# A decoder block on one Trainium2 core: weaving column chunks at stage seams, sums moved from GpSimd to VectorE, and a new order of the sine tables

## The chip, the cores and the metric

The kernel runs on one core of a Trainium2 chip. The core has a matmul engine (TensorE, PE in the profile, with its weight loads PEld), VectorE (DVE), ScalarE (ACT), GpSimd (POOL) and a queue engine for transfers (SP). Each engine works through its own instructions in order and waits on semaphores for the others. The metric is device time in microseconds, the median of several runs; lower is better.

## The reference

One layer of a hybrid decoder block, with batch 1, 256 tokens, width 2048, all in float32:

```
xn   = rms_norm(x)
proj = xn @ w_in                      # 2048 x 11264: u_s5, u_lru, q, k, v, gate logits
g_s5, g_lru, g_attn = split(sigmoid(gate_logits + b_gate))
y_s5   = s5_branch(u_s5, ...)         # complex diagonal scan, gelu, y * sigmoid(y @ w_glu + b)
y_lru  = rglru_branch(u_lru, ...)     # causal conv, two gates, h = a*h + sqrt(1-a^2)*(i*x)
y_attn = stick_breaking_attention(q, k, v)
merged = g_s5*(y_s5 @ w_br_s5) + g_lru*(y_lru @ w_br_lru) + g_attn*(y_attn @ w_br_attn)
h   = x + merged @ w_out
hn  = rms_norm(h)
h   = h + relu(hn @ w_up)**2 @ w_down # width 8192 between
out = rms_norm(h)
```

The S5 branch turns each state by a phase that grows with the time step, so it needs tables of sines and cosines. Its output matrix C is multiplied beforehand with a factor that depends on the parameters ("C's folding").

## The kernel before, in words

**Weight stream.** All large matrices pass through one stream of units, written out by hand at the top (`stream`, lines 61 to 94). A unit is 256 rows by 512 columns, 512 KB. Each unit is loaded by SP (`load_next`, L119) and split in two parts in a reduced float format, the high part by a cast on ScalarE (L135), the rest by a subtraction on VectorE (L136). A matrix with K rows gives K/256 units for a chunk of 512 columns: eight for 2048 rows, four for 1024. `next_unit` (L140) keeps loads three units and splits two units ahead of use; three buffers exist for the raw unit and three for the split one.

**Chunks.** `chunk` (L184) computes 512 columns with channels on the partitions, 24 matmuls of 256 columns a unit; `chunk_tok` (L204) does it with tokens on the partitions, 12 matmuls of 512 columns a unit. In both each product is three matmuls (high by high, and two with a low part). A chunk fills two of the four PSUM banks that are tagged for this.

**Woven work.** Everything else is written as Python generators, registered with `later(gens, rate)` (L153). After every unit `pump` (L168) advances each registered generator by `rate` steps. What it issues is ordered behind the unit's last matmul and behind the newest split on each engine (`anchor`). `finish(task)` issues all steps that are left at once. The order on each engine is settled by the framework's scheduler, which mostly follows the order of issue.

**Stages.** In order:

- Eight-unit chunks of w_in for the RG-LRU input (chunks 2, 3), then S5's input (0, 1). Woven in are the first norm (`norm1`, L316), S5's parameters (`s5_params`, L366, on GpSimd, with C's folding in L421 to 431) and the RG-LRU parameters and halves (`lru_params` L460, `lru_half` L477, through one task `lq` at one step a unit).
- Four times a gate chunk and a chunk of w_br_lru (`gate_branch(1, ...)`, L720). From here on the S5 scan is woven in (`s5_scan`, L585, 1.27 steps a unit), in eight blocks. Each block needs a sine and a cosine table (`s5_tables`, L549): a sum on VectorE (L558), a rounding on ScalarE and VectorE (L560, L561), then Abs, Sin and Sin with a shift (L563 to L565). Sigmoid, Exp, Sqrt and Sin need different function tables on ScalarE, which an ACT_TABLE_LOAD brings.
- Chunks for q, k, v with attention woven in, then four gate chunks and four chunks of w_br_attn.
- S5's gate chunks, w_glu and w_br_s5. `gates` (L690) adds the gate's bias and takes the sigmoid (L699), `branch` (L703) multiplies; for the second and third branch the sum into `merged` is on GpSimd (L711).
- Four chunks of w_out. Before them the merged tokens are transposed in 32x32 blocks on VectorE (`blocks`, L679; `split_tok`, L848), chunk after chunk; the last one (L870) runs while w_out's first chunk is under way, at two steps a unit, and must be done when its unit 6 begins (`ms`, L876). After each chunk `residual` (L886) transposes and splits the result for the next stage; the second norm (`norm2`, L907) follows the last one.
- Four quarters of the MLP, each four chunks of w_up (2048 to 512 columns) and four chunks of w_down (K = 2048). After each w_up chunk ScalarE takes the relu (L986), and `hidden` (L967) transposes (four steps of four blocks), squares on ScalarE and GpSimd, and subtracts (L974). The last chunk of a quarter runs this at two steps a unit, because w_down's unit 6 needs it (`hs_`, L990).

`finish` inside `ms`, `hs` and `hs_` is what forces the remaining steps when the twelfth block of rows (kt >= 12, unit 6) is reached.

## Time and profile before

| what | value |
|---|---|
| median of 3 runs | 1529.46 us (1527.65 to 1530.21) |
| the profiled execution's own time | 1528.9 us |
| its span, first to last instruction | 1527.0 us |
| TensorE, VectorE, ScalarE, GpSimd busy | 1491.6, 1170.1, 780.2, 113.2 us |
| mean granted TensorE clock | 0.993 |
| read from HBM | 282.71 MB, 187 GB/s over the span |

How to read the profile: it shows one execution. A group of instructions is given as line, engine, operation, written and read tiles, count, then total busy time and mean duration in ns, then the engine's idle time just before these instructions and what ended it. A wait is given as the waiting engine and line, the releasing engine and line, then the total, the number of times and the longest. TensorE's busy share counts matmuls that overlap in its pipeline, so the distance between the starts of two matmuls says more than the duration of one. The row for a stretch of time gives the busy time of the engines in it and the granted clock, 1.00 being full speed.

### The profile page before, as it was taken

The numbers are of one execution on the slowest core, as the hardware profiler recorded it, in microseconds if no ns is written. First come the engines' busy times: TensorE is split into PE (matmuls) and PEld (weight loads), VectorE is DVE, ScalarE is ACT, GpSimd is POOL, SyncE is SP. The second block draws the span as 40 slices with busy tenths as digits, with TensorE's granted clock in tenths as the row PEclk, the third lists the DMA queues.
The fourth block names the chain that finished last, engine by engine and source line by source line (L and its number), as shares of the span: only waits on it lengthen the run. The fifth ranks groups of instructions, "written<-read, shape, count | busy, mean of one in ns | idle before, by whom it ended". The sixth has DMA issues, their size and how long they took to land.

```text
span 1527.0 us, 19937 instructions
## 1 busy us (share of the span) xinstructions
PE 1491.6 (98%) x7518; PEld 1261.0 (83%) x7518; DVE 1170.1 (77%) x1428; ACT 780.2 (51%) x918; POOL 113.2 (7%) x100
## 2 busy tenths in 40 slices
PE   9898999999998999999999999999999999999997
PEld 9896888989887877987788878888788887888786
DVE  5886998897988989688889885568754886558855
ACT  7478556565765564544346443344433443344443
POOL 6300000000000100001000000000100000000111
PEclk9999999999999999999999999999999999999999
DMA  9454766665565756665765656656566666666564
GB/s 290 143 173 143 227 209 193 194 184 167 172 184 168 209 184 204 187 203 182 250 200 184 184 181 210 191 187 193 193 193 193 192 194 186 195 187 198 176 203 152
DMA packets 88914, 292.41 MB, mean 191 GB/s; under 512 B 12786, under 2 KB 17010, under 8 KB 88562
## 3 DMA queue, kind: packets, MB, share of 16 engines
q1 hardware_dynamic: 88386, 287.93, 60.9%
q10 hardware_dynamic: 432, 3.21, 0.6%
q8 instruction: 59, 0.97, 0.3%
q14 instruction: 37, 0.30, 0.1%
HBM read 282.71 MB, written 2.10 MB: 187 GB/s over the span
## 4 chain that ended last, share of the span: by engine, by line
PE 83%; DVE 9%; ACT 3%; issue 3%; DMA 2%; SPq 0%; DVEq 0%; ACTq 0%
PE mt_w_up L215 7%; PE mt_w_up L214 7%; PE mt_w_up L213 7%; PE mt_w_down L214 7%; PE mt_w_down L215 7%; PE mt_w_down L213 7%; PE mt_w_in L214 5%; PE mt_w_in L215 5%; PE mt_w_in L213 5%; PE mm_w_in L198 4%; PE mm_w_in L199 4%; PE mm_w_in L197 4%; DVE lo L136 4%; ACT hi L135 2%; DVE reluT L683 1%
## 5 line engine op out<-in xcount | busy, mean ns | idle before, releaser
L136 DVE TENSOR_TENSOR lo<-raw,hi 128x1024 fp32r<-128x1024 f32 (+1 forms) x521 | 657.2, 1265 | 305.9 <-ACT hi L135 297.1
L135 ACT CAST hi<-raw 128x1024 fp32r<-128x1024 f32 (+1 forms) x521 | 545.5, 1049 | 643.3 <-PE mt_w_down L215 165.3
L214 PE MATMUL mt_w_down<-lo,hd_hi 128*128 128x512 f32 (+1 forms) x528 | 202.5, 384 | 5.6 <-DVE lo L136 5.6
L213 PE MATMUL mt_w_down<-hi,hd_hi 128*128 128x512 f32 (+1 forms) x528 | 202.1, 383 | 0.0
L215 PE MATMUL mt_w_down<-hi,hd_lo 128*128 128x512 f32 (+1 forms) x528 | 202.0, 383 | 0.0
L214 PE MATMUL mt_w_up<-lo,hhi 128*128 128x512 f32 x512 | 199.3, 389 | 0.0
L215 PE MATMUL mt_w_up<-hi,hlo 128*128 128x512 f32 x512 | 199.2, 389 | 0.0
L213 PE MATMUL mt_w_up<-hi,hhi 128*128 128x512 f32 x512 | 199.2, 389 | 0.0
L214 PE MATMUL mt_w_in<-lo,xhi 128*128 128x512 f32 x448 | 176.3, 394 | 4.2 <-DVE lo L136 4.1
L213 PE MATMUL mt_w_in<-hi,xhi 128*128 128x512 f32 x448 | 177.3, 397 | 2.9 <-ACT hi L135 2.9
L215 PE MATMUL mt_w_in<-hi,xlo 128*128 128x512 f32 x448 | 175.3, 391 | 0.0
L199 PE MATMUL mm_w_in<-xhi,lo 128*128 128x256 f32 x512 | 145.8, 286 | 3.1 <-DVE lo L136 3.0
L197 PE MATMUL mm_w_in<-xhi,hi 128*128 128x256 f32 x512 | 146.3, 286 | 1.7 <-DVE rs L298 0.9
L198 PE MATMUL mm_w_in<-xlo,hi 128*128 128x256 f32 x512 | 145.8, 285 | 0.0
L214 PEld LDWEIGHTS mt_w_down<-lo,hd_hi 128*128 128x128 f32 x528 | 99.2, 188 | 26.6 <-DVE lo L136 7.3
L213 PEld LDWEIGHTS mt_w_down<-hi,hd_hi 128*128 128x128 f32 x528 | 99.2, 188 | 19.5
L215 PEld LDWEIGHTS mt_w_down<-hi,hd_lo 128*128 128x128 f32 x528 | 99.2, 188 | 19.3
L683 DVE STREAM_TRANSPOSE reluT<-relu 32x256 f32<-32x256 f32 x256 | 111.5, 436 | 4.1
L214 PEld LDWEIGHTS mt_w_up<-lo,hhi 128*128 128x128 f32 x512 | 96.1, 188 | 20.1
L213 PEld LDWEIGHTS mt_w_up<-hi,hhi 128*128 128x128 f32 x512 | 96.1, 188 | 19.9
L215 PEld LDWEIGHTS mt_w_up<-hi,hlo 128*128 128x128 f32 x512 | 96.1, 188 | 19.9
L214 PEld LDWEIGHTS mt_w_in<-lo,xhi 128*128 128x128 f32 x448 | 84.6, 189 | 25.0 <-DVE lo L136 8.6
(278 smaller groups left out, 2039.5 us busy)
## 6 DMA issues: line engine op xcount, KB each, us to landing
raw<-in_w_in SPq DMA_DIRECT2D x175, 512.0 KB, 4.1
raw<-in_w_up SPq DMA_DIRECT2D x128, 512.0 KB, 4.0
raw<-in_w_down SPq DMA_DIRECT2D x128, 512.0 KB, 4.3
raw<-in_w_out SPq DMA_DIRECT2D x32, 512.0 KB, 4.3
raw<-in_w_br_lru SPq DMA_DIRECT2D x16, 512.0 KB, 4.2
raw<-in_w_br_attn SPq DMA_DIRECT2D x16, 512.0 KB, 4.1
raw<-in_w_br_s SPq DMA_DIRECT2D x16, 512.0 KB, 4.1
stk<-ux SPq DMA_DIRECT2D x96, 64.0 KB, 3.9
```

The costliest lines, as they stand in the source:

```text
L135: anchor["act"] = nc.scalar.copy(h[:, k, :], r[:, k, :]).ins
L136: anchor["dve"] = nc.vector.tensor_tensor(l_[:, k, :], r[:, k, :], h[:, k, :].bitcast(F32), ALU.subtract).ins
L197: nc.tensor.matmul(o, wh[:, kk, s], xh, start=first and ct % 2 == 0, stop=False, skip_group_check=True)
L198: nc.tensor.matmul(o, wh[:, kk, s], xl, start=False, stop=False, skip_group_check=True)
L199: mm = nc.tensor.matmul(o, wl[:, kk, s], xh, start=False, stop=last and ct % 2 == 1, skip_group_check=True)
L213: nc.tensor.matmul(banks[j], xh[:, s], wh[:, a:b], start=kt == 0, stop=False)
L214: nc.tensor.matmul(banks[j], xh[:, s], wl[:, a:b], start=False, stop=False)
L215: return nc.tensor.matmul(banks[j], xl[:, s], wh[:, a:b], start=False, stop=kt == ng * UK - 1)
L683: nc.vector.transpose(d_[32 * a:32 * a + 32, :, :, 32 * b:32 * b + 32], s_[32 * b:32 * b + 32, :, :, 32 * a:32 * a + 32])
```

## The change

Six things are changed.

1. **Woven seams.** A new function `pair_tok` computes two chunks of 512 columns together: units 0 to 5 of the first, units 0 to 5 of the second, then units 6 and 7 of the first, and of the second. It takes all four PSUM banks. It is used for the first two chunks of w_out, of the first quarter's w_up, and of w_down in all four quarters; the stream is written to match. The three tasks at the seams (`split_tok(3)`, the residual of w_out's last chunk, `hidden` of a quarter's last chunk) run at one step a unit instead of two.
2. **Branch sums on VectorE.** L711's `m + g` moves from GpSimd to VectorE: 16 instructions of 128x512.
3. **C's folding on VectorE.** The eight instructions L424, L426 and L430 move from GpSimd to VectorE.
4. **Sine and cosine together.** The cosine's activation is kept in `anchor["sin"]`. All ScalarE work that is woven in later, and the gate sigmoids, are ordered behind it.
5. **First S5 table early.** Block 0's table is made at the end of `s5_params` instead of at the start of `s5_scan`. The tables, the parameters and the second part of an RG-LRU half now share the tag "tab", two buffers of the same total size as the four before.
6. **More RG-LRU steps.** The task `lq` runs at 1.25 steps a unit instead of 1.

```
+    LATE = 2
+    def add_pair(name, c, k, g0=0):
+        ng = k // (P * UK)
+        for gs_ in (range(ng - LATE), range(ng - LATE, ng)):
+            stream.extend((name, c + i, g0 + g) for i in range(2) for g in gs_)
+    add_pair("w_out", 0, D)
...
+        if q == 0:
+            add_pair("w_up", 0, D)
...
+        add_pair("w_down", 0, FQ, q * (FQ // (P * UK)))
...
+    def pair_tok(name, c, k, xs, done):
+        ng = k // (P * UK)
+        banks = [[psm.tile([P, CH], F32, tag="mm", ...) for t in range(2)] for i in range(2)]
+        for gs_ in (range(ng - LATE), range(ng - LATE, ng)):
+            for i in range(2):
+                for g in gs_:
+                    (nm, cc, _), wh, wl = next_unit()
...
+                    anchor["pe"] = mm.ins
+                    pump()
+                if gs_.stop == ng:
+                    done(c + i, banks[i])
...
-            g.tensor_tensor(u[:, 0], cco[:, 0], p, ALU.mult)
+            nc.vector.tensor_tensor(cq[:, 0], cco[:, 0], p, ALU.mult)
...
+        tabs, more = s5_tables(0)
+        tab0.append(tabs)
+        yield from more
...
-    lq = later([lru_params()], 1)
+    lq = later([lru_params()], 1.25)
...
-            nc.scalar.activation(cf, cf, AF.Sin, scale=-TURN, bias=half_pi)
+            anchor["sin"] = nc.scalar.activation(cf, cf, AF.Sin, scale=-TURN, bias=half_pi).ins
...
-            nc.scalar.activation(g, g, AF.Sigmoid)
+            with tc.issue_after(anchor["sin"]):
+                nc.scalar.activation(g, g, AF.Sigmoid)
...
-                nc.gpsimd.tensor_tensor(m, m, g, ALU.add)
+                nc.vector.tensor_tensor(m, m, g, ALU.add)
...
-    last = later([split_tok(3, ...)], 2.0)
+    last = later([split_tok(3, ...)], 1.0)
...
-        rq = later([residual(c)], 2.0 if c == 3 else 1.0)
+        rq[0] = later([residual(c)], 1.0)
...
+    pair_tok("w_out", 0, D, ms, out_done)
...
-            hq = later([hidden(...)], 2.0 if c == FQ // CH - 1 else 1.0)
+            hq[0] = later([hidden(...)], 1.0)
...
+        if q == 0:
+            pair_tok("w_up", 0, D, hs, up_done)
...
+        pair_tok("w_down", 0, FQ, hs_, down_done)
```

`out_done`, `up_done` and `down_done` hold what stood behind a chunk before: emptying the banks and registering the woven task.

## Prediction

> **What bounds the kernel now.** I read the page first (busy time, groups), then the waits of TensorE, then the busy time by stretch, and last the timeline at the places where TensorE waits.

> ```profile
> span 1527.0 us, 19937 instructions
> PE 1491.6 (98%) x7518; PEld 1261.0 (83%) x7518; DVE 1170.1 (77%) x1428; ACT 780.2 (51%) x918; POOL 113.2 (7%) x100
> L136 DVE TENSOR_TENSOR lo<-raw,hi 128x1024 fp32r<-128x1024 f32 (+1 forms) x521 | 657.2, 1265 | 305.9 <-ACT hi L135 297.1
> ```

> TensorE is busy for 98% of the span, and the change takes no matmul away. So the gain can only come from its waits, and from the stretches with a lowered clock that follow them. A stretch without waits gives the pace:

> ```profile
> 916.00:1078.00 162.00, 162.00 (x716) 134.17 (x715) 106.28 (x120) 69.17 (x70) 6.96 (x4) 1.00 0.62 196
> 900.00:916.00 16.00, 14.60 (x65) 11.78 (x64) 13.26 (x22) 7.59 (x9) 1.64 (x1) 1.00 0.51 162
> 56.00:64.00 8.00, 7.41 (x33) 7.02 (x33) 3.64 (x9) 1.89 (x4) 0.00 (x0) 0.57 0.57 182
> 133.00:150.00 17.00, 12.61 (x49) 9.25 (x47) 12.15 (x18) 13.90 (x22) 0.00 (x0) 0.90 0.48 154
> 480.00:500.00 20.00, 17.63 (x79) 13.47 (x81) 15.20 (x16) 13.32 (x14) 2.34 (x2) 0.91 0.44 143
> ```

> (Columns: stretch, length, busy PE, PEld, DVE, ACT, POOL with counts, granted clock, DMA share, GB/s.) 162 us / 716 gives 0.226 us for a matmul, so 2.72 us for a unit of 12. Each unit needs its split ready in time: one cast on ScalarE, one subtraction L136 on VectorE. The granted clock falls in three places and costs 8 x 0.43 = 3.4, 17 x 0.10 = 1.7 and 20 x 0.09 = 1.8 us. At 900 to 916, with a wait of 1.4 us, it stays at 1.00.

> TensorE's waits, asked by stretch (38 to 64, 117 to 160, 440 to 620, 690 to 850; the last row is from the whole run):

> ```profile
> PE mm_w_in L199 <- DVE lo L136: 2.4, 2, 1.3
> PE ps_n L322 <- DVE xT L313: 1.6, 1, 1.6
> ...
> PE mt_w_in L213 <- ACT hi L135: 2.7, 1, 2.7
> PE mt_w_br_lru L213 <- ACT hi L135: 1.1, 1, 1.1
> PE mt_w_br_lru L214 <- DVE lo L136: 0.5, 1, 0.5
> PE mt_w_in L214 <- DVE lo L136: 0.5, 1, 0.5
> ...
> PE mt_w_in L214 <- DVE lo L136: 2.3, 3, 1.5
> PE mt_w_br_attn L213 <- ACT hi L135: 2.2, 1, 2.2
> ...
> PE mt_w_out L214 <- DVE lo L136: 2.4, 3, 1.5
> PE mt_w_in L214 <- DVE lo L136: 1.3, 1, 1.3
> PE ps_n L914 <- DVE hT L313: 0.9, 1, 0.9
> ...
> PE mt_w_down L214 <- DVE lo L136: 5.6, 4, 1.4
> ```

> These sum to 23.5 us, with the clock 30.4. That is about all that this change can win. The start and the tail are not touched.

> **C's folding on VectorE.** Rows of the folding, and of VectorE with and without it:

> ```profile
> 38.00:56.00 18.00, 14.30 (x113) 13.48 (x112) 16.59 (x10) 7.89 (x8) 14.92 (x10) 1.00 0.48 148
> 32.37 1.23 DVE L136 TENSOR_TENSOR lo<-raw,hi 128x1024 fp32r<-128x1024 f32 x1 [3.23 <-ACT hi L135]
> 43.27 2.32 DVE L136 TENSOR_TENSOR lo<-raw,hi 128x1024 fp32r<-128x1024 f32 x1
> 54.22 0.68 DVE L313 TENSOR_TENSOR xT<-xT 128x512 f32<-128x512 f32 x1
> ```

> While POOL folds (14.92 of these 18 us), L136 takes 2.32 instead of 1.23. VectorE's ten instructions, eight of 128x1024 and two smaller, would need about 8 x 1.23 + 0.68 = 10.5 us; they took 16.6. So the folding costs VectorE 6.1 us. On VectorE itself it is eight instructions of 512 elements a lane, 8 x 0.68 = 5.4 us. The load hardly falls, but it comes in pieces of 0.68, one a unit. The three waits behind the first norm (2.4, 1.6) and the clock after them (3.4) sum to 7.4 us. Against that stand two table steps of 1.21 us that now follow, and the RG-LRU convolution:

> ```profile
> 64.00:75.00 11.00, 10.27 (x79) 10.09 (x80) 10.71 (x21) 5.49 (x8) 0.00 (x0) 1.00 0.32 93
> 75.00:95.00 20.00, 20.00 (x163) 19.79 (x162) 12.49 (x16) 18.08 (x29) 0.00 (x0) 1.00 0.50 161
> L561 DVE SCALAR_TENSOR_TENSOR ts<-ts,tc 128x1024 f32<-128x1024 f32 x8 | 9.7, 1214 | 0.0
> ```

> VectorE is full from 64 to 75 (10.71 of 11), and TensorE would arrive there some 7 us sooner. I take **5.5 us gained**, from 0 (the waits move there) to 7.4.

> **First table early, 1.25 steps a unit.** At 127 to 135 ScalarE's cast is 8.3 us late (next fence): loads, sine, cosine and the RG-LRU exponentials stand between two casts.

> ```profile
> 126.90 1.05 ACT L135 CAST hi<-raw 128x1024 fp32r<-128x1024 f32 x1
> 127.97 1.28 ACT L564 ACT_TABLE_LOAD   x1
> 135.17 2.92 ACT L135 CAST hi<-raw 128x1024 fp32r<-128x1024 f32 x3
> L565 ACT ACTIVATE tc<-tc,half_pi 128x1024 f32<-128x1024 f32 x8 | 9.1, 1136 | 0.0
> ```

> Load, sine and cosine are about 3.5 of the 8.3; 4.8 is left, under two units (5.4), so this wait goes. At 1.25 steps a unit the second RG-LRU half (14 steps) ends near unit 35, ahead of the branch at unit 40, where its last steps were flushed. All of 2.7, 1.1, 0.5, 0.5 and the clock's 1.7 go: 6.5 us. But the table (four passes of about 1.1, two loads of 1.28: 7.0 us) is now cast among units 18 to 20, just where the first RG-LRU half brings sigmoid, exponential and root closer together. ScalarE is idle for 5.5 us of 64 to 75 and 1.9 of 75 to 95, 7.4 in all. It just fits on paper, so I charge 2 us of new waits: **4.5 gained**, from -2 (the wait of 133 is only moved, and grows) to 6.5. The scan itself starts three steps, 2.4 units, earlier; nothing waits for that.

> **Sine and cosine together.**

> ```profile
> 480.72 1.28 ACT L564 ACT_TABLE_LOAD   x1
> 483.08 1.28 ACT L699 ACT_TABLE_LOAD   x1
> 485.54 1.28 ACT L565 ACT_TABLE_LOAD   x1
> ```

> A gate's sigmoid stands between sine and cosine, and three loads follow each other. With the new order one load of each kind is left, 2.6 us less, more than the wait of 2.2 behind it; with the clock, **4.0 gained**, from 0 to 4.2. The added order makes gate sigmoids and all woven ScalarE work wait for the cosine, which waits for L561 on VectorE; behind them on ScalarE are casts. Their lead of two units hides 1.2 us of that; it does not hide a VectorE that is more than a unit behind.

> **Branch sums on VectorE.** Eight columns, two adds each.

> ```profile
> L711 POOL TENSOR_TENSOR merged<-merged,gate 128x512 f32<-128x512 f32 x16 | 28.3, 1789 | 645.3 <-DMA raw<-in_w_in 404.8 <-DVE gate L710 240.5
> 460.34 2.32 DVE L625 TENSOR_TENSOR t<-t,s_v 128x1024 f32<-128x1024 f32 x1
> 500.00:612.00 112.00, 111.17 (x533) 90.07 (x522) 103.18 (x108) 62.79 (x73) 8.25 (x5) 1.00 0.66 202
> ```

> The adds cost VectorE 2 x 0.68 = 1.4 us a column. They take away POOL's 2 x 1.79 = 3.6 us, in which an instruction like L625 loses 1.1 us (2.32 against 1.21); one to two fall into it. The balance is between -0.3 and +0.8 us a column, on an engine that is 92% busy here. I take **0**, from -11 (sixteen adds in full, 16 x 0.68) to +3.6 (the waits 2.3 and 1.3 go).

> [...]

> **Woven seams.** Today the last chunk's transposes run at two steps a unit and must be done after six units.

> ```profile
> 904.68 3.57 DVE L683 STREAM_TRANSPOSE reluT<-relu 32x256 f32<-32x256 f32 x8
> L884 DVE SCALAR_TENSOR_TENSOR hlo<-hT,par,hhi 128x256 fp32r<-128x256 f32 x16 | 6.9, 478 | 0.0
> ```

> A unit with eight transposes asks VectorE for 1.23 + 3.57 = 4.80 us in 2.72, 2.08 too much. Two such units, 4.2 us too much, made the wait of 1.4 at each down seam: the lead absorbs 2.8. At one step a unit a unit asks 1.23 + 1.79 = 3.02; four of them are 1.2 too much and are absorbed, with twelve units of time for seven steps. So **5.6 gained** at the four down seams (4 to 5.6), **2.0** of 2.4 at the first w_out chunk, and **0.9** at the second norm's sum, whose steps no longer meet the doubled rate.

> The weave has a price. In a pair both chunks end within two units of each other, and two tasks of four transposes a unit run together, once in w_out and once in the first w_up. In w_out two units are 2.08 over, then two have 1.23 + 1.79 + 2 x 0.48 = 3.98, 1.26 over: 6.7, less the lead 2.8, is 3.9 us. In w_up, two units are 2.08 over and two 0.3, with L974 behind: 4.8 - 2.8 = 2.0. **5.9 lost**, from 0 (the queue finds gaps) to 11.5 (no lead left). The down pairs have no such tasks.

> At nothing: the loads are the same 520 in another order; a pair takes all four banks, but its second chunk needs the banks before it six units (16 us) late, and emptying is two instructions of 0.7; the tiles' new tags hold the same bytes.

> **Sum.** 5.5 + 4.5 + 4.0 + 0 + 5.6 + 2.0 + 0.9 - 5.9 = 16.6 us. The profiled execution took 1528.9 (its span 1527.0 and 1.9 around it), 0.6 under the median 1529.46. 1529.5 - 16.6 is **1513 us**.

> **Rivals.** *The front only moves its waits*: folding and table give 1 and -2 instead of 5.5 and 4.5, since VectorE (64 to 75) and ScalarE (75 to 95) are full where the work goes. 16.6 - 11.0 = 5.6: 1524 us. For it: those rows. Against it: the wait at 127 has two loads and a table in it that nothing brings back there. *The weave is free and the front gains whole*: 16.6 + 5.9 + 1.9 + 2.0 = 26.4, 1503 us. Against it: the row of eight transposes in a block. *The sine order changes nothing*, because the queue would have placed the sigmoid elsewhere anyway once all has shifted: 4.0 less, 1517 us. *VectorE becomes the bound from 458 to 730* (slower): the sixteen adds fall on TensorE in full, 10.9 us, and a wait at each of eight branch ends reaches the size that lowered the clock at 480 to 500 (2.2 us; 1.4 did not), 8 x 1.8 = 14.4. Together 25.3 against 16.6: 9 us slower, 1538 us. It decides if the wait at most branch ends passes 2 us. For it: 103 of 112 busy; against it: POOL's collisions end in the same places.

> [...]

> **Chances.** Forecast 0.55, moved waits 0.17, free weave 0.16, idle sine order 0.05, VectorE bound 0.07. A measurement of this kernel can tell about 0.2%, 3 us, from no change. The forecast, the free weave and the sine case are faster (with 0.01 kept back), and some two thirds of the moved waits: 0.86; same 0.07, slower 0.07. The range reaches from the free weave less 3 us of unknown to the moved waits and 2 more: 1500 to 1526.

> **What would show it.** Right: POOL with 16 plus 8 instructions fewer, no DVE instruction of 2.1 to 2.3 us from 40 to 56; clock 1.00 from 56 to 64 and 133 to 150; never a sigmoid load between sine and cosine; no mt_w_down wait at the four seams; new L136 waits of some 4 and 2 us late in the w_out and w_up pairs. Wrong: waits on the cast near 65 to 90; L136 waits over 2 us at branch ends with a lowered clock; down seams that still wait.

## The result and the profile after

The changed kernel takes 1534.78 us (median of 6 runs, 1534.36 to 1535.68) beside 1528.99 for the kernel before (6 runs, 1527.65 to 1530.21). The ratio is 1.0037 with a 95% interval of 1.0028 to 1.0047: 5.8 us slower, where 16.6 us faster had been forecast. The profiled execution took 1534.64, its span 1532.8 at a mean granted clock of 0.990 (before: 1528.9, 1527.0, 0.993).

The head of the page, then TensorE's waits over the whole run:

```profile
span 1532.8 us, 19925 instructions
PE 1495.9 (98%) x7518; PEld 1263.8 (82%) x7518; DVE 1170.7 (76%) x1452; ACT 779.8 (51%) x918; POOL 65.8 (4%) x76
```

```profile
PE mm_w_in L208 <- DVE rs L331: 4.2, 1, 4.2
PE mt_w_in L224 <- ACT hi L146: 4.0, 2, 2.7
...
PE mt_w_up L225 <- DVE lo L147: 3.3, 1, 3.3
PE mt_w_out L225 <- DVE lo L147: 2.5, 2, 1.8
```

The instruction counts are as forecast (POOL 24 fewer), and the four waits of 1.4 us at the down seams are gone. In their place stand waits of more than 3 us that were not there before: on the norm's result, and on the split behind the w_up pair. A third kind stands among S5's scan blocks (on a cast, 2.7 us at the longest). Two stretches of the prediction, and those of the other waits:

```profile
56.00:64.00 8.00, 3.78 (x21) 3.61 (x20) 7.33 (x18) 3.28 (x6) 0.00 (x0) 0.69 0.57 178
133.00:150.00 17.00, 15.19 (x63) 12.07 (x62) 10.03 (x13) 9.16 (x14) 0.00 (x0) 0.90 0.64 206
420.00:440.00 20.00, 16.75 (x76) 12.50 (x75) 12.16 (x14) 14.24 (x17) 0.00 (x0) 0.91 0.34 103
786.00:796.00 10.00, 8.16 (x29) 6.23 (x29) 9.77 (x18) 4.30 (x8) 0.00 (x0) 0.83 0.38 119
873.00:887.00 14.00, 10.67 (x35) 8.18 (x34) 13.65 (x21) 4.95 (x5) 2.67 (x2) 0.76 0.43 128
```

The clock (third number from the right) is lowered in each of them. From 56 to 64 it was 0.57 and is 0.69, but TensorE is busy for only 3.78 of the 8 us; at 133 it is as low as before. Where the time came from is read off the first matmul of each stage in the timeline, as the difference to the kernel before (two kernels of the experiments stand beside it):

| stage begins | before | changed | without weave | scan held |
|---|---|---|---|---|
| w_out | 722.72 | +3.1 | +1.8 | -2.7 |
| w_up | 813.09 | +6.9 | +1.1 | +0.4 |
| first w_down | 901.77 | +12.6 | +1.5 | +5.7 |
| span | 1527.0 | +5.8 | +7.3 | -1.2 |

Each column is one profiled execution; that of the kernel with the scan held took 1527.61 us, 1.4 under its median (1528.98).

In the changed kernel the front lost 3.1 us (forecast: 14.0 gained), w_out 3.8 and the first w_up 5.7 (forecast: 3.0 lost by the two together, 5.9 less 2.0 and 0.9), and the four down seams gave 6.8 back (forecast: 5.6). So of the 22.4 us by which the forecast missed, 17.1 lie in the front and 6.5 in the two pairs, less 1.2 at the seams.

### The profile page after: what moved, and what is told of

The parts are those of the page before. It is cut to its first block, busy times and chain, and to the rows that moved or that the text cites. A ratio compares the mean times of both kernels' runs of the same rounds, so it can differ in the third digit from the quotient of the medians.

```text
span 1532.8 us, 19925 instructions
## 1 busy us (share of the span) xinstructions
PE 1495.9 (98%) x7518; PEld 1263.8 (82%) x7518; DVE 1170.7 (76%) x1452; ACT 779.8 (51%) x918; POOL 65.8 (4%) x76
## 4 chain that ended last, share of the span: by engine, by line
PE 77%; DVE 10%; ACT 5%; DMA 4%; issue 3%; SPq 1%; DVEq 0%; ACTq 0%
PE mt_w_up L225 6%; PE mt_w_up L226 6%; PE mt_w_up L224 6%; PE mt_w_in L225 5%; PE mt_w_in L226 5%; PE mt_w_in L224 5%; DVE lo L147 4%; PE mp_w_down L261 4%; PE mp_w_down L259 4%; PE mp_w_down L260 4%; PE mt_w_down L225 4%; PE mt_w_down L224 4%; PE mt_w_down L226 4%; DMA raw<-in_w_in 3%; PE mm_w_in L210 2%
## 5 line engine op out<-in xcount | busy, mean ns | idle before, releaser
L226 PE MATMUL mt_w_up<-hi,hlo 128*128 128x512 f32 x448 | 175.4, 392 | 0.0
L224 PE MATMUL mt_w_up<-hi,hhi 128*128 128x512 f32 x448 | 175.2, 391 | 0.0
L208 PEld LDWEIGHTS mm_w_in<-xhi,hi 128*128 128x128 f32 x512 | 99.2, 194 | 7.0 <-issue 4.4
L210 PEld LDWEIGHTS mm_w_in<-xhi,lo 128*128 128x128 f32 x512 | 98.3, 194 | 6.0 <-DVE lo L147 6.0
L224 PEld LDWEIGHTS mt_w_in<-hi,xhi 128*128 128x128 f32 x448 | 84.5, 189 | 21.8 <-ACT hi L146 4.6
L225 PE MATMUL mt_w_down<-lo,hd_hi 128*128 128x512 f32 (+1 forms) x272 | 102.5, 377 | 0.0
L224 PE MATMUL mt_w_down<-hi,hd_hi 128*128 128x512 f32 (+1 forms) x272 | 102.4, 377 | 0.0
L226 PE MATMUL mt_w_down<-hi,hd_lo 128*128 128x512 f32 (+1 forms) x272 | 102.4, 376 | 0.0
L260 PE MATMUL mp_w_down<-lo,hd_hi 128*128 128x512 f32 x256 | 99.6, 389 | 0.0
L259 PE MATMUL mp_w_down<-hi,hd_hi 128*128 128x512 f32 x256 | 99.6, 389 | 0.0
```

Source lines behind the costliest of these rows:

```text
L208: nc.tensor.matmul(o, wh[:, kk, s], xh, start=first and ct % 2 == 0, stop=False, skip_group_check=True)
L210: mm = nc.tensor.matmul(o, wl[:, kk, s], xh, start=False, stop=last and ct % 2 == 1, skip_group_check=True)
L224: nc.tensor.matmul(banks[j], xh[:, s], wh[:, a:b], start=kt == 0, stop=False)
L225: nc.tensor.matmul(banks[j], xh[:, s], wl[:, a:b], start=False, stop=False)
L226: return nc.tensor.matmul(banks[j], xl[:, s], wh[:, a:b], start=False, stop=kt == ng * UK - 1)
L259: nc.tensor.matmul(o, xh[:, s], wh[:, kk, :], start=kt == 0, stop=False)
```

## The experiments

Seventeen kernels, each timed in five rounds beside the kernel before on the same chip. "Alone" means one part of the change put on the kernel before.

| kernel | what it has | us | ratio, 95% interval |
|---|---|---|---|
| w_down | pairs at the down seams alone | 1521.67 | 0.9958, 0.9946 to 0.9971 |
| w_all | all woven seams alone | 1531.99 | 1.0020, 1.0011 to 1.0029 |
| w_seq | w_all, second task behind the first | 1529.32 | 1.0003, 0.9994 to 1.0012 |
| w_serial | w_all, never two tasks in a unit | 1527.21 | 0.9987, 0.9978 to 0.9995 |
| fold | folding on VectorE alone | 1525.63 | 0.9982, 0.9973 to 0.9990 |
| fold_late | the same, eight units later | 1520.95 | 0.9948, 0.9935 to 0.9960 |
| sums | branch sums alone | 1527.38 | 0.9986, 0.9977 to 0.9995 |
| sine | sine order alone | 1529.25 | 0.9999, 0.9990 to 1.0007 |
| rate | 1.25 steps alone | 1529.09 | 1.0001, 0.9992 to 1.0009 |
| table | early first table alone | 1535.43 | 1.0040, 1.0028 to 1.0053 |
| table_rate | table and rate | 1542.00 | 1.0086, 1.0072 to 1.0100 |
| fold_table_rate | fold, table and rate | 1535.55 | 1.0050, 1.0036 to 1.0063 |
| table_hold | table, the scan held | 1526.54 | 0.9985, 0.9976 to 0.9994 |
| no_weave | whole change without the weave | 1535.92 | 1.0048, 1.0035 to 1.0061 |
| after_hold | whole change, the scan held | 1528.98 | 1.0003, 0.9994 to 1.0012 |
| best_b | w_down, fold_late, sums | 1512.16 | 0.9891, 0.9875 to 0.9906 |
| best_c | best_b and table_hold | 1507.22 | 0.9862, 0.9847 to 0.9877 |

The kernel before had a median of 1528.35 to 1529.02 in these comparisons.

### The seams: w_down and w_all

w_down keeps w_out and w_up as they were; only the pairs of w_down are woven, and the last chunk of each w_up runs at one step a unit.

```diff
-        for c in range(4):
+        add_pair("w_down", 0, FQ, q * (FQ // (P * UK)))
+        for c in range(2, 4):
...
-            hq = later([hidden(...)], 2.0 if c == FQ // CH - 1 else 1.0)
+            hq[0] = later([hidden(...)], 1.0)
```

> The kernel before with only the w_down pairs woven, and the hidden task of a quarter's last chunk at one step a unit; w_out and w_up as before. Theory: the waits of 1.4 to 1.7 us at four seams go and nothing comes instead: 6 to 7 us faster, about 1522. Rival (the pair's order or the slower task costs as much elsewhere): within 2 us of before.

w_all has the pairs of w_out and the first w_up as well (the change's parts 1 and 2 whole).

> The kernel before with the woven seams alone (w_out, first w_up, all w_down), nothing else changed. Theory: four down seams gain 6.8 us, and the doubled transposes behind the two pairs of w_out and w_up lose 3.8 and 5.7 as in the trace of after: 2.7 us slower than before, about 1531.7. Rival (the weave is good, the whole loss comes from the front half): some 7 us faster, 1522.

w_down gains 7.0 us, w_all loses 3.3. So the pairs in w_out and w_up cost some 10 us between them. VectorE's timeline in the changed kernel shows how, behind the w_up pair:

```profile
864.73 1.78 DVE L722 STREAM_TRANSPOSE reluT<-relu 32x256 f32<-32x256 f32 x4
...
867.80 3.58 DVE L722 STREAM_TRANSPOSE reluT<-relu 32x256 f32<-32x256 f32 x8
871.41 1.23 DVE L147 TENSOR_TENSOR lo<-raw,hi 128x1024 fp32r<-128x1024 f32 x1
872.67 3.61 DVE L722 STREAM_TRANSPOSE reluT<-relu 32x256 f32<-32x256 f32 x8
876.31 2.68 DVE L147 TENSOR_TENSOR lo<-raw,hi 128x1024 fp32r<-128x1024 f32 x1
```

(Columns: start, duration, engine, line, operation.) Two tasks of four transposes fall into one unit twice, as forecast, and the second subtraction then takes 2.68 instead of 1.23, because GpSimd squares the hidden values (L1016, from 876.02 to 877.91) beside it. TensorE waits 3.3 us, and the clock is 0.76 from 873 to 887.

The w_out pair had been promised 2 us at its first chunk. Little of that came: TensorE's waits there, 1.54 and 0.28 us before, are 1.05 and 0.76 in w_all and 0.28 and 0.76 in the changed kernel. ScalarE's cast there in the changed kernel:

```profile
738.80 1.05 ACT L146 CAST hi<-raw 128x1024 fp32r<-128x1024 f32 x1 [6.24 <-DMA raw<-in_w_out]
```

and ScalarE's waits of the kernel before, 725 to 745:

```profile
ACT hi L135 <- DMA raw<-in_w_out: 7.3, 2, 7.1
```

The cast waits for its weights in both, while the residual input (2048 KB, issued at 729.27) is loaded. In the kernel before the 1.54 us still ended on a subtraction behind eight transposes (734.47), but the next unit's weights landed only for the cast at 736.48. With the transposes out of the way, what ends last there is that transfer, and the rate of VectorE's transposes does not move it.

### The seams: w_seq and w_serial

Both keep the pairs and take the doubled tasks away. w_seq puts the second chunk's task behind the first; w_serial lets every task wait for the one before it.

```diff
-        rq[0] = later([residual(c)], 1.0)
+        if c == 1 and rq[0] in side:      # w_serial: without "c == 1 and"
+            rq[0][0].append(residual(c))
+        else:
+            rq[0] = later([residual(c)], 1.0)
```

(and the same for `hidden`)

> As the kernel with all seams woven, but in the pairs of w_out and w_up the second chunk's woven task is queued behind the first one's, so that no unit has eight transposes. Theory (the price of the pairs is two tasks in one unit on VectorE): the L136 waits in w_out's third chunk and w_up's third chunk go, 8 to 10 us faster than before, about 1520. Rival (the pairs cost through banks or the order of use): about 2.7 us slower than before, like the kernel with two tasks.

> All seams woven, and in w_out and w_up every chunk's task is queued behind the one before, so that two of them never share a unit (with only the pairs queued, the third chunk's task met the second's, and the waits came back at 804 and 902). Theory (the price of the pairs is the overlap of two tasks on VectorE): the waits late in w_out and w_up go; with four seams gained 6.8 us that is 6 to 8 us faster, about 1522. Rival (the pairs cost by themselves): within 2 us of before, or slower.

w_seq came to 1529.3, not 1520: the second task, now late, met that of the third chunk. Its VectorE timeline:

```profile
799.94 1.23 DVE L147 TENSOR_TENSOR lo<-raw,hi 128x1024 fp32r<-128x1024 f32 x1
801.20 3.61 DVE L717 STREAM_TRANSPOSE hT<-h_tok 32x256 f32<-32x256 f32 x8
```

Eight transposes stand together again, a chunk later than in the changed kernel (783.60). w_serial has no such block, and behind the first chunk of w_out its largest wait there is 0.4 us; it gains 1.8, 5.2 less than w_down. A task then runs in nearly every unit, 1.23 + 1.79 = 3.02 against 2.72 us, and its profiled execution still loses 2.1 us in w_up (from 811.17 to 901.92: 90.75, before 88.68). The doubled block was a real cost, but pairing two chunks whose woven tasks are this dense did not pay in any of the three orders that were run.

### The folding: fold and fold_late

fold only takes C's folding from GpSimd to VectorE. fold_late also lets eight units pass first, which puts it behind the first norm.

```diff
-            g.tensor_tensor(u[:, 0], cco[:, 0], p, ALU.mult)
+            nc.vector.tensor_tensor(u[:, 0], cco[:, 0], p, ALU.mult)
...
+        for _ in range(8):                # fold_late only
+            yield
         cb_, ib_ = (x.unsqueeze(2)...)
```

> The kernel before with only C's folding on VectorE. Theory: the doubled L136 goes, but TensorE then waits for a PSUM bank behind the chain from the first norm, which folding steps stretch; the waits near 50 to 64 are replaced, the time stays within 2 us of before. Rival (the folding is a gain and the early table behind it spoils it in the changed kernel): 4 to 7 us faster.

> The kernel before with C's folding on VectorE and started eight units later, behind the first norm. Theory (two folding steps and the casts between them stretch the chain from the norm's sum to the first scaled bank): the bank wait of 4.2 us shrinks to about 2, some 2 us faster than with the folding in place, 1523.5. Rival (TensorE simply arrives sooner and the chain is as long as it was): wait of about 4, 1525.6 as with the folding in place.

fold gains 3.1 us, fold_late 8.1. First fold's VectorE, then fold_late's, at the norm:

```profile
54.93 0.42 DVE L297 SCALAR_TENSOR_TENSOR rs<-rs 128x256 f32<-128x256 f32 x1
55.28 0.68 DVE L430 TENSOR_TENSOR ce<-cq 64x512 f32<-64x512 f32 x1
55.88 0.41 DVE L298 SCALAR_TENSOR_TENSOR rs<-ps_n,rs 128x256 f32<-128x256 f32 x1
56.88 1.23 DVE L136 TENSOR_TENSOR lo<-raw,hi 128x1024 fp32r<-128x1024 f32 x1 [0.59 <-ACT hi L135]
58.02 0.42 DVE L299 SCALAR_TENSOR_TENSOR rstd<-rs,rs 128x256 f32<-128x256 f32 x1
58.48 0.69 DVE L430 TENSOR_TENSOR ce<-cq 64x512 f32<-64x512 f32 x1
...
59.27 0.68 DVE L340 TENSOR_TENSOR ulru<-mm_w_in,rstd 128x512 f32<-128x512 f32 x1
```

```profile
54.87 0.42 DVE L298 SCALAR_TENSOR_TENSOR rs<-ps_n,rs 128x256 f32<-128x256 f32 x1
55.33 0.42 DVE L299 SCALAR_TENSOR_TENSOR rstd<-rs,rs 128x256 f32<-128x256 f32 x1
55.79 0.69 DVE L340 TENSOR_TENSOR ulru<-mm_w_in,rstd 128x512 f32<-128x512 f32 x1
```

In fold the subtraction takes 1.23 us, so the contention with GpSimd is gone, as forecast. But folding steps (L430) and a subtraction that waits 0.59 for its cast stand between the norm's steps L297, L298 and L299, and the first scaled bank (L340), which TensorE needs back, is emptied at 59.27. In fold_late it is at 55.79, 3.5 us sooner. Their stretches of 56 to 64, fold and then fold_late:

```profile
56.00:64.00 8.00, 3.90 (x18) 3.93 (x19) 7.34 (x17) 3.09 (x6) 0.00 (x0) 0.69 0.48 142
```

```profile
56.00:64.00 8.00, 7.37 (x61) 7.40 (x62) 8.00 (x18) 4.61 (x8) 0.00 (x0) 1.00 0.16 47
```

The wait of 4.2 us and the lowered clock behind it go; a wait of 1.3 us is left. With the folding on VectorE the kernel is 3.1 us faster inside the norm's chain and 8.1 behind it.

### Sums, sine order and rate alone

```diff
-                nc.gpsimd.tensor_tensor(m, m, g, ALU.add)      # sums
+                nc.vector.tensor_tensor(m, m, g, ALU.add)
...
-            nc.scalar.activation(g, g, AF.Sigmoid)             # sine
+            with tc.issue_after(anchor["sin"]) if "sin" in anchor else ExitStack():
+                nc.scalar.activation(g, g, AF.Sigmoid)
...
-    lq = later([lru_params()], 1)                              # rate
+    lq = later([lru_params()], 1.25)
```

> The kernel before with only the branch sums on VectorE. Theory (POOL's collisions cost as much as the adds): the L136 waits of 1.5, 0.4 and 0.5 us at 463, 545 and 573 go, 1 to 3 us faster. Rival (VectorE is full there and every add falls on TensorE): 3 to 11 us slower.

> The kernel before with only sine and cosine ordered ahead of later functions. Theory (the order binds only what is woven in later; an older exponential of the attention can still fall between the two): the wait at 486 goes, but another pair may be split; 0 to 4 us faster. Rival (woven work waits for a late sine, casts behind it): slower by 1 to 4 us.

> The kernel before with only 1.25 RG-LRU steps a unit. Theory (the second RG-LRU half ends before its branch, so the flush and its waits of 1.1 and 0.5 at 148 go, but sigmoid, exponential and root come closer in both halves): 0 to 3 us faster. Rival (closer steps load ScalarE and VectorE in units 16 to 32): 2 to 4 us slower.

The sums gain 1.6 us, within the forecast's bounds of -11 and +3.6. The sine order and the rate change nothing that can be measured. In the sine kernel a sigmoid still stands between sine and cosine:

```profile
479.94 1.28 ACT L564 ACT_TABLE_LOAD   x1
482.31 1.28 ACT L700 ACT_TABLE_LOAD   x1
484.76 1.28 ACT L565 ACT_TABLE_LOAD   x1
```

`anchor["sin"]` names the last cosine that had been issued when the sigmoid was issued. A sigmoid that was issued before this block's cosine waits only for an older one, and the scheduler may still place it between the two. The order binds what comes later, and the wait came from what was already there. The rival in which the sine order changes nothing was right in its effect, not in its reason: the sigmoid had not moved elsewhere. In the changed kernel the wait at 489 is gone (the clock from 480 to 500 is 1.00), and in `table`, without the order, it is gone too. In after_hold, with the order, it is back with 2.2 us, and a sigmoid's load again splits the pair. So it went with the scan's earlier start, not with the order.

### The early table: table, table_rate and table_hold

table makes block 0's table at the end of `s5_params`; table_rate adds the 1.25 steps; table_hold lets the scan pass three of its steps before it begins, as many as the table took there before.

```diff
+        tabs, more = s5_tables(0)          # end of s5_params
+        tab0.append(tabs)
+        yield from more
...
-        tabs, more = s5_tables(0)          # start of s5_scan
-        yield from more
+        tabs = tab0[0]
+        for _ in range(3):                 # table_hold only
+            yield
```

> The kernel before with only the first table made early and the shared tiles. Theory (ScalarE's block of sine, exponentials and loads is moved from 127 to about 78, not dissolved): the wait of 2.7 at 133 goes, waits of some 2 to 4 us come near 80 to 105; within 3 us of before. Rival (the forecast's view, the idle time of 7.4 us there takes it in): 4 to 5 us faster.

> The early table and 1.25 steps together, nothing else. Theory (the two meet in units 17 to 21 and cost there what neither costs alone; subtracting the other measured parts from the changed kernel leaves about 7 us slower for these two): 3 to 7 us slower than before. Rival (they add up): the sum of the two single runs, expected between 3 faster and 3 slower.

> The first S5 table early, but the scan then idles for three of its steps, so its eight blocks begin where they began before the change. If the 6.5 us of the early table come from the blocks that now start 2.4 units sooner and meet the attention at 188 and 430, this gives back about 4 of them: some 1531. If they come from the table's own place among units 18 to 20, where the cast waits 12 us on ScalarE, nearly nothing comes back: 1534 to 1536, with the waits near 85 and 95 still there and those near 430 gone.

table costs 6.5 us and table_rate 13.1, both more than either side had expected. The cause is not where the table is made. table_hold makes it in the same place and is 2.2 us faster than before: the 8.8 us between table (+6.5) and table_hold (-2.2, each to its own runs of before) come from the scan's start alone. table, 180 to 200 and 420 to 440, then table_hold:

```profile
180.00:200.00 20.00, 18.31 (x73) 14.28 (x71) 16.34 (x17) 12.90 (x13) 0.00 (x0) 0.91 0.54 166
420.00:440.00 20.00, 17.19 (x73) 13.53 (x73) 12.90 (x15) 16.01 (x18) 0.00 (x0) 0.91 0.30 90
```

```profile
180.00:200.00 20.00, 20.00 (x89) 16.49 (x89) 19.78 (x23) 14.45 (x15) 0.00 (x0) 1.00 0.66 202
420.00:440.00 20.00, 20.00 (x94) 16.68 (x92) 17.68 (x19) 12.74 (x16) 0.00 (x0) 1.00 0.45 140
```

Every later block of the scan begins 2.4 units sooner and meets other woven work. At 420 that is the attention's exponential (L799), as ScalarE of the changed kernel shows:

```profile
421.52 1.28 ACT L799 ACT_TABLE_LOAD   x1
...
423.35 1.28 ACT L417 ACT_TABLE_LOAD   x1
...
425.82 1.28 ACT L799 ACT_TABLE_LOAD   x1
```

Before, sine and cosine stood side by side here behind one load:

```profile
423.99 1.06 ACT L564 ACTIVATE ts<-ts 128x1024 f32<-128x1024 f32 x1
424.95 1.13 ACT L565 ACTIVATE tc<-tc,half_pi 128x1024 f32<-128x1024 f32 x1
```

Now an exponential splits them, with two loads more, and the casts behind them are late: TensorE waits 2.7 us, until 429.77. The early start also removes waits. By its stage starts `table` is 12.9 us behind the kernel before at the first chunk of w_br_attn and 8.0 at w_out, because the waits of 1.5 and 2.2 us at 465 and 489, and the lowered clock behind the second, are gone. What a shift costs depends on what each block happens to meet.

The place of the table itself is not free either: in table_hold TensorE waits once for a cast there (2.5 us, until 88.12). That is near the 2 us that the prediction had charged, but it left out the clock behind it: 0.69 from 84 to 95 in this execution, which costs 3.4 us more. With 1529.5 us it was the slowest of the eleven of table_hold, so this need not happen each time.

Of the 6.6 us that table_rate takes beyond `table`, little lies where the 1.25 steps act: at the start of w_out the two are 8.9 and 8.0 us behind the kernel before. From the first w_down to the end table_rate loses 5.2 us more and `table` nothing. The code of the down seams is the same, but TensorE waits 1.86 us at each in table_rate and 1.40 in `table`.

### What stands together: fold_table_rate, no_weave and after_hold

fold_table_rate and no_weave put parts of the change together without new lines; after_hold is the changed kernel with the three steps of table_hold.

> C's folding on VectorE together with the early table and 1.25 steps a unit; no weave, sums on GpSimd, old sine order. The single runs add to +13.1 - 3.1 = +10, so 1539. If folding on VectorE also takes the strain from the stretch in which the table is made, because the table then no longer comes behind a GpSimd folding that ends late, the two together cost less than that: +1 to +5, 1530 to 1534.

> The whole change but for the woven seams. The stage starts of the changed kernel put this part at +2.9 us and the weave behind it at +2.9, so 1532. If the two parts are independent of each other, this is also after's 5.8 less the weave's own 3.3: 1531.4. If it came out at the sum of the single runs, 1537.5, the weave would have to gain 3 us in the changed kernel where it lost 3.3 alone.

> The changed kernel with one edit: the S5 scan idles for three of its steps, so its blocks begin 2.4 units later, about where they began before the change. The hold gave the early table alone 8.7 us back (from +6.5 to -2.2). If the scan's early start is what spoils the changed kernel, the wait of 2.7 at 426 goes and the stretches from 160 to 200 and from 420 to 500 come back: 1534.8 less 5 to 8, 1527 to 1530. If its start is harmless in this company (1.25 steps a unit, sums on VectorE, new sine order), 1533 to 1536.

fold_table_rate costs 6.8 us (1535.55 against 1528.78) where the single kernels add to 10.0: the folding on VectorE is worth 6 beside the early table and 3 alone (3.9 of the 6 by the start of w_out, the rest at the down seams). Neither expectation was met, as it lies between the two. no_weave costs 7.1 us, and the changed kernel 5.8: beside this front the weave is worth about 1 us, where alone it costs 3.3. The reason is in no_weave's four down seams. ScalarE at its second, and the stretches around the first two:

```profile
1082.86 1.05 ACT L135 CAST hi<-raw 128x1024 fp32r<-128x1024 f32 x1 [0.24 <-DMA raw<-in_w_down]
```

```profile
912.00:922.00 10.00, 7.89 (x26) 6.05 (x27) 8.06 (x13) 3.13 (x4) 2.91 (x1) 0.83 0.45 155
1090.00:1100.00 10.00, 8.24 (x37) 6.50 (x36) 8.09 (x13) 4.10 (x4) 2.91 (x1) 1.00 0.49 157
```

The code there is that of the kernel before, but a cast waits for its weights a little longer, the transposes start about 0.35 us later, and TensorE's wait of 1.40 becomes 1.66 to 1.86; at the first and the third seam the clock now falls to 0.83. By the table of the stage starts the four seams cost 5.8 us more than before (+7.3 at the end against +1.5 at the first w_down). The paired seams of the changed kernel have no such wait, so they save more in this company. Why the weights land later there, and in table_rate, is not settled.

after_hold takes 1528.98, 0.6 over before's 1528.35: the scan's early start costs the whole change 5.2 of the 5.8 us that it lost. Its column in the first table shows the rest plainly: 2.7 us gained in the front, 8.4 lost in the two pairs, 6.9 gained at the seams.

### The parts that pay: best_b and best_c

best_b joins w_down, fold_late and sums; best_c adds table_hold.

> The parts that paid: w_down pairs alone, C's folding on VectorE behind the first norm, branch sums on VectorE. Theory (they lie in different stretches and add up: 7.0 + 8.1 + 1.6): 16 to 17 us faster than before, about 1512. Rival (what one part frees is lost at the next wait): 10 us faster or less.

> The parts that paid: the paired down seams, the folding on VectorE behind the norm, the sums on VectorE, and the early table with the held scan; no pairs in w_out and w_up, one RG-LRU step a unit, old sine order. If the held table's 2.2 us add to the other parts as those added to each other: 1510. If the table's place among units 18 to 20 meets the folding that now runs eight units later on VectorE, they are lost: 1512 to 1515.

best_b gains 16.7 us, the sum of its parts (7.0 + 8.1 + 1.6), best_c 21.1, more than its sum of 18.9. TensorE's waits in best_c, all that sum to 1 us or more:

```profile
PE mt_w_br_attn L221 <- ACT hi L143: 2.2, 1, 2.2
PE mt_w_in L222 <- DVE lo L144: 1.9, 2, 1.5
PE mm_w_in L207 <- DVE lo L144: 1.6, 3, 0.7
PE mm_w_in L205 <- DVE rs L328: 1.3, 1, 1.3
PE mt_w_out L222 <- DVE lo L144: 1.1, 2, 0.8
PE warm L310 <- POOL ones L307: 1.0, 1, 1.0
```

best_c is faster than both kernels of this case by 21 and 27 us, with the change's own parts: without the two dense pairs, the folding moved behind the norm, and the scan held where it was.

## Why the prediction was wrong

The prediction's reading of what bounds the kernel held: there were some 23 us of waits and 7 of lowered clock to win, and best_c won 21 us of the two together. Its sum failed at these steps.

**The scan's earlier start.** "The scan itself starts three steps, 2.4 units, earlier; nothing waits for that." This step alone holds 5.2 of the 5.8 us that the change lost. The prediction had priced the moved table, but put at nothing what every later step of the task does when it comes 2.4 units sooner. table against table_hold (8.8 us) and the changed kernel against after_hold (5.2) show its price. The gain of the table itself was 2.2 of the 4.5 forecast. The 1.25 steps brought nothing alone. On top of the early table they came with 6.6 us more, of which some 5 lie in the down seams, where nothing was changed; how one leads to the other stays open.

**The price of the pairs.** For w_out and w_up 5.9 us lost and 2.9 won had been forecast, 3.0 lost; w_all against w_down puts it at 10.3. Of that, 2.0 is what the first w_out chunk did not give (with the transposes gone, a transfer ended last there). The place and the doubled transposes were right, the sizes of the waits were not: 2.5 us in w_out where 3.9 had been forecast, 3.3 in w_up where 2.0 had been. Missing were the clock behind them (0.83 and 0.76 in the changed kernel) and GpSimd's square beside the subtraction.

**The folding.** The contention went as told, but of 5.5 us came 3.1. The prediction's lower end, "the waits move there", had the right form with the wrong place: the steps did not crowd VectorE from 64 to 75 but stood inside the norm's own chain. What the contention cost in the kernel before shows in these rows:

```profile
39.20 1.06 POOL L426 TENSOR_TENSOR cq<-cco,prm 128x512 f32<-128x512 f32 x1
40.22 2.04 POOL L424 TENSOR_TENSOR cq<-cco,prm 128x512 f32<-128x512 f32 x1
39.41 1.93 DVE L136 TENSOR_TENSOR lo<-raw,hi 128x1024 fp32r<-128x1024 f32 x1 [1.52 <-PE mm_w_in L198]
```

A folding step alone is 1.06 us. L136 starts inside one (39.20 to 40.26) and ends 1.08 us behind it; the next step starts inside L136, lasts 2.04 and ends 0.92 behind that. So of its 1.93 us, 1.23 alone, L136 lost 0.70 here, and of the 2.32 at 43.27 it lost 1.09, as much as a whole step: as if the two engines took turns.

**The sine order.** 4.0 us forecast, 0 measured; the rival with 0.05 had the effect right by luck, as its reason did not hold. The prediction listed "never a sigmoid load between sine and cosine" as a sign without asking from which issue onward the order binds.

**What held.** The down seams: 5.6 forecast, 6.8 in the changed kernel and 7.0 alone. The sums: 0 within wide bounds, 1.6 measured; VectorE did not become the bound.

The rival in which the front only moves its waits named the right part, at 11 us less than forecast; the front fell 17 short of its 14.0. With the scan held, the single kernels add to a gain of 3.2 (fold 3.1, table_hold 2.2, sums 1.6, sine and rate -0.2 each, w_all -3.3), and after_hold loses 0.6; these 4 us are not assigned to a part. The 1.25 steps beside a held table were not run alone. That the seams' gain grows beside a worse front shows that the parts do not simply add.

## What to carry to other kernels

When a step is taken out of a task that advances with the units, everything behind it in the task moves too: ask of each later block what it will meet, or hold the task's place with empty steps. When work is moved to the engine that carries a short chain to a full buffer, count what lands between the links of that chain; the same eight instructions were worth 3 us inside a norm's chain and 8 behind it. Weave two pieces of work only where the woven tasks behind them are thin, and price a wait of some 2 us or more with the lowered clock that may follow (1.7 us behind the 2.2 at 489 in the kernel before).

## What the runs showed of the hardware

Whether the clock falls after a wait is not settled by the wait's length alone. In table_rate TensorE waits 1.86 us at each of the four down seams; the first and the last:

```profile
918.00:928.00 10.00, 8.13 (x35) 6.20 (x34) 8.06 (x13) 4.10 (x4) 2.91 (x1) 1.00 0.48 156
1448.00:1458.00 10.00, 8.02 (x28) 5.83 (x27) 8.06 (x13) 3.10 (x4) 2.91 (x1) 0.83 0.51 143
```

```profile
1450.50:1453.90 3.40, 1.54 (x8) 0.95 (x7) 3.33 (x6) 1.63 (x2) 0.43 (x1) 1.00 0.25 100
1453.90:1457.30 3.40, 3.40 (x10) 2.63 (x9) 1.61 (x2) 0.36 (x1) 2.48 (x1) 0.50 0.80 198
```

Here the whole wait lies in one step; at the first seam two steps share it, and the larger part is 1.72 us. For a forecast this means that a wait near 1.9 us has two prices: alone, or with a drop of one step, which at half speed costs another 1.7 us.

A change of ScalarE's function table cost 1.28 us and no more between two functions (the load at 423.35 in the changed kernel ends at 424.63, and its cosine begins at 424.64).
